# State space layer with tokens in (step, chunk) order, a buffer of its own for u's evictions, and two weight copies behind the first gelu parts

## The chip, the cores and the metric

The kernel runs on one core of a Trainium2 chip. The time is device microseconds of one execution; 1237.46 us is the median of three runs before (1236.57 to 1237.71). The profile is that of one further execution. TensorE is PE in its rows (its weight load PEld), VectorE DVE, ScalarE ACT, GpSimd POOL; SP is the engine that issues most of the DMAs.

## What is computed

The network has two blocks of two layers and one token batch of 256 by 1024 fp32. Only the first layer, a state space mixer, is touched. It projects to u and z, runs a complex diagonal recurrence over the 256 tokens for each of 64 groups, and gates the result:

```python
proj = h @ w_in
u, z = proj[..., :SSM_WIDTH], proj[..., SSM_WIDTH:]
...
y = y.reshape(bsz, seq, SSM_WIDTH) + d_skip.astype(jnp.float32) * uf
y = jax.nn.gelu(y)
y = y * jax.nn.sigmoid(y @ w_glu.astype(jnp.float32) + b_glu.astype(jnp.float32))
y = y.astype(h.dtype) * jax.nn.silu(z)
return y @ w_out
```

The product with `w_glu` is called the unit here.

## The kernel before

The layer is the method `s5`, the first 160 us of the program. All activations are kept transposed, with 128 channels on the partitions and the 256 tokens along the free axis. The 256 tokens are 64 chunks (index j) of 4 steps (index t), and token number 4j + t stands at place 4j + t.

x is transposed and scaled into `hT` (L657 on DVE, L660 on ACT). `gemm_raw` and `block` (L428, L726) form u and z with unsplit fp32 weights. `ev_u` (L695) multiplies each of u's eight blocks by the row factor `rsb`, turns its tokens from (j t) to (t j), and puts it into a `pg` tile; of these the stage has four. Line 696 stores the block to a DRAM buffer `s5ud`, and `load_u` (L735) reads it back as `s5U`, with steps and channels on the partitions: four loads for channels 0 to 511, four for the rest. From `s5U` PE forms the states' inputs (L796), ACT puts them into `s5V` (L799), and DVE runs the recurrence for the first half of the groups and then for the second (L818 to L844), leaving `s5Xc`.

For each half h, PE forms the output (L857, L874), ACT copies it to `s5Y` (L880, the result copy), eight DMAs store it to `s5yd` (L884), and two loads (L893) bring it back with channels on the partitions. The loop over `b` makes of each load a gelu part: gelu on ACT (L896) into `s5gf`, its fp32r high half `s5gh` on ACT (L901), the low half `s5gl` on DVE (L903), both written in the order (j t) from (t j). There are four parts: 1 and 2 from the first half, 3 and 4 from the second.

A weight of the unit comes as eight tiles of 256 by 512. `wtile` makes each ready: a load (L149), the high copy `hi` on ACT (L158), the low copy `lo` on DVE (L160). Tiles 1 and 2 and tiles 3 and 4 are multiplied with parts 1 and 2, tiles 5 and 6 with part 3, tiles 7 and 8 with part 4 (`gemm_t`, L454 to L456). Tiles 1 to 4 are prepared in the branch `if h == 0` that stands ahead of the loop over the parts. The evacuation `ev_glu` (L916 to L921) forms the gated value m, `split` (L193, L194) its halves `s5mh` and `s5ml`, and `out_rows` multiplies by `w_out` (L165 to L167); its weight tiles w1 to w8 pass through `wtile` too.

Each engine and each DMA queue works in the order of issue. `issue_after` sets where in its own engine's order an instruction stands; what it needs from others is waited for by semaphores.

Of the kernel before, what the change touches and what calls it, by code (L numbers as in the profile page):

```python
# [23 lines left out]
C = 512  # L24
KT = 2
# [25 lines left out]
class Net:  # L51
# [570 lines left out]
    def s5(self, x_in):  # L622
        nc, I = self.nc, self.I
        tt = nc.vector.tensor_tensor
        s5p = self.ctx0.enter_context(self.tc.tile_pool(name="s5p", bufs=1))
        dp = self.ctx0.enter_context(self.tc.tile_pool(name="s5d", bufs=1, space=DRAM))
        ud = dp.tile([1024, 256], F32, name="s5ud")
# [44 lines left out]
        zs = [self.xp.tile([128, 4, 256], F32, tag="x", name=self.nm("s5z")) for _ in range(2)]  # L672
# [4 lines left out]
        rsb = self.sp.tile([128, 256], F32, tag="s5rsb", name="s5rsb", bufs=1)  # L677
# [9 lines left out]
        def spread_r():  # L687
            p = self.small()
            with self.tc.issue_after(self.last_raw.ins):
                nc.tensor.matmul(p[:, :256], ones, dg.rearrange("p t n -> p (t n)"), start=True, stop=True)  # L690
            nc.scalar.activation(rsb, p[:, :256], AF.Copy)

        def ev_u(b, p):
            d = self.tmp([128, 4, 64], "s5u")
            self.last_u = tt(d, p.rearrange("p (j t) -> p t j", t=4), rsb.rearrange("p (j t) -> p t j", t=4), op=ALU.mult)  # L695
            nc.sync.dma_start(ud[b * 128:(b + 1) * 128, :], d.rearrange("p t j -> p (t j)"))

        def ev_z(b, p):
            nc.scalar.activation(zs[b // 4][:, b % 4], p, AF.Copy)
# [76 lines left out]

        V = s5p.tile([128, 4096], F32, tag="s5X", name="s5V").rearrange("p (h g q i n) -> p h g q i n", h=2, q=2, i=2, g=4)

        Xc = s5p.tile([128, 2, 2, 2, 8, 65], F32, name="s5Xc")
        nc.gpsimd.memset(Xc[:, :, :, :, :, 0:1].rearrange("p h q c a o -> p (h q c a) o"), 0.0)  # L780
        zg = deque()
        for h in range(2):
# [1 line left out]
        for q in range(2):  # L784
# [84 lines left out]
        for h in range(2):  # L869
# [13 lines left out]
                    r = q * 64 + t * 16  # L883
                    nc.sync.dma_start(yv[q, t][:, 16 * h:16 * h + 16], Y[h][r:r + 16].rearrange("p a g j -> p (a g) j"))  # L884
            if h == 0:
                self.split_after = ly, ls
                order = (0, 4, 2, 6)
                Wg = I["ssm_w_glu"][0]
                for k0, n0 in list(itertools.product(order, (0, C)))[:4]:
                    self.pre.append(self.wtile(Wg[k0 * 128:(k0 + KT) * 128, n0:n0 + C], KT, C, False))  # L890
            for b in (2 * h, 2 * h + 4):
                y = self.tmp([128, 2, 4, 64], "s5y")
                nc.sync.dma_start(y.rearrange("p b t j -> p b (t j)"), yw[:, b:b + 2])  # L893
                i = b % 4
                g = gf[b // 4][:, i:i + 2]
                nc.scalar.activation(g, y, AF.Gelu_apprx_tanh)  # L896
                gh, gl = gT[b // 4]
                if b == 6:
                    lg0, ll0 = lg, ll
                nat = lambda a: a[:, i:i + 2, :].rearrange("p b (j t) -> p b t j", t=4)  # L900
                lg = nc.scalar.activation(nat(gh), g, AF.Copy)  # L901
                with self.tc.issue_after(ls.ins):
                    ll = nc.vector.tensor_tensor(nat(gl), g, nat(gh).bitcast(F32), op=ALU.subtract)  # L903
        self.split_after = lg0, ll0
        for h in range(2):
            with self.tc.issue_after(ll.ins):
# [7 lines left out]
        def ev_glu(b, p):  # L914
            th = self.tmp([128, 256], "s5th")
            nc.scalar.activation(th, p, AF.Tanh, bias=hb[:, b:b + 1], scale=0.5)  # L916
            m = self.tmp([128, 256], "s5mm")
            nc.vector.tensor_tensor(m.rearrange("p (j t) -> p t j", t=4), gf[b // 4][:, b % 4],
                                    zs[b // 4][:, b % 4].rearrange("p (j t) -> p t j", t=4), op=ALU.mult)
            nc.vector.scalar_tensor_tensor(m, zt[b // 4][:, b % 4], 1.0, m, op0=ALU.add, op1=ALU.mult)  # L920
            nc.vector.scalar_tensor_tensor(m, th, 1.0, m, op0=ALU.add, op1=ALU.mult)  # L921
            mh, ml = (a[:, b % 4, :] for a in mT[b // 4])
            self.split(mh, ml, m, 0.25)
        zt = [self.page([128, 4, 256], "s5zt") for _ in range(2)]

        def tanh(h):
# [599 lines left out]
```

## Time and profile before

| | before |
|---|---|
| median of three runs | 1237.46 us |
| the profiled execution, its own time | 1238.92 us |
| its span, first to last instruction | 1237.1 us |
| PE busy | 1205.6 us (97%) |
| DVE busy | 927.1 us (75%) |
| ACT busy | 669.2 us (54%) |
| granted TensorE clock, mean | 0.991 |

The span is the time from the first to the last instruction; the execution's own time has 1.8 us around it. A share of busy time is a mean over stages with different limits, so what the state space layer's 160 us hang on is read from its own stretch of the timelines. A timeline row gives the start in us, the length, engine and line, operation, output and inputs, how many instructions it merges, and in brackets how long the engine stood idle before it and whom it waited for.

### The profile page before, as it was taken

Reading aid. Unit: us, or ns where it says so; the run is one execution under the profiler, and the core shown is the slowest. Engines: PE = TensorE matmul, PEld = TensorE weight load, DVE = VectorE, ACT = ScalarE, POOL = GpSimd, SP = SyncE. Lnnn points to the kernel's source line nnn. Section 1 sums busy time; section 2 is a strip of 40 time slices with the busy share of each in tenths; the row PEclk is TensorE's granted clock in tenths of the full one; section 3 lists DMA queues with packets and bytes.
Section 4 is the critical chain, followed back from the end, with each engine's and each line's share of the span. In section 5 each row is a group of like instructions: output and inputs, shape, how many; then the busy total and the mean of one; then the engine's idle time right before and its main releaser. Section 6 shows DMA issues by size and latency. Waiting matters only on the chain.

```text
span 1237.1 us, 17677 instructions
## 1 busy us (share of the span) xinstructions
PE 1205.6 (97%) x6438; PEld 1000.9 (81%) x6438; DVE 927.1 (75%) x1856; ACT 669.2 (54%) x1137; POOL 8.3 (1%) x29
## 2 busy tenths in 40 slices
PE   7997999999999999999999999999999999999997
PEld 6886887878887888887888887887788887888886
DVE  8895989786899997767654546899998866655544
ACT  5214677765767545446544535668545546544541
POOL 0100000000000000000000000000000000000000
PEclk9898999999999999999999999999999999999999
DMA  8664575443654554663764763744544563765661
GB/s 310 132 95 137 179 225 184 153 141 100 199 167 126 167 170 154 188 204 102 254 188 146 242 204 95 229 136 143 182 146 161 179 210 104 241 192 156 216 201 49
DMA packets 125367, 210.58 MB, mean 170 GB/s; under 512 B 22113, under 2 KB 31329, under 8 KB 125281
## 3 DMA queue, kind: packets, MB, share of 16 engines
q1 hardware_dynamic: 121344, 205.29, 54.0%
q10 hardware_dynamic: 3936, 4.18, 1.1%
q8 instruction: 50, 0.82, 0.3%
q14 instruction: 37, 0.30, 0.1%
HBM read 205.83 MB, written 3.60 MB: 169 GB/s over the span
## 4 chain that ended last, share of the span: by engine, by line
PE 79%; DVE 11%; DMA 4%; ACT 3%; issue 2%; SPq 1%; DVEq 0%; ACTq 0%
PE mm L165 23%; PE mm L167 23%; PE mm L166 23%; DVE lo L160 2%; PE sm L203 2%; ACT hi L158 1%; DVE s5f L818 1%; PE sm L1266 1%; DVE cacc L1018 1%; PE sm L1155 1%; PE sm L1186 1%; DVE s5V L840 1%; PE sm L796 1%; DMA s5bc<-in_c_s 1%; DMA s5ud<-pg 1%
## 5 line engine op out<-in xcount | busy, mean ns | idle before, releaser
L160 DVE TENSOR_TENSOR lo<-raw,hi 128x1024 fp32r<-128x1024 f32 (+2 forms) x372 | 439.9, 1187 | 225.0 <-ACT hi L158 220.6
L158 ACT ACTIVATE hi<-raw 128x1024 fp32r<-128x1024 f32 (+2 forms) x372 | 382.4, 1033 | 358.5 <-PE mm L167 291.0
L165 PE MATMUL mm<-hi,xTh 128*128 128x512 f32 (+2 forms) x1152 | 449.7, 393 | 1.7 <-ACT xTh L193 1.5
L167 PE MATMUL mm<-hi,xTl 128*128 128x512 f32 (+2 forms) x1152 | 442.2, 385 | 0.3 <-DVE t L297 0.2
L166 PE MATMUL mm<-lo,xTh 128*128 128x512 f32 (+2 forms) x1152 | 442.2, 384 | 0.2 <-DVE lo L160 0.2
L165 PEld LDWEIGHTS mm<-hi,xTh 128*128 128x128 f32 x1152 | 216.6, 188 | 49.6 <-ACT xTh L193 7.3
L167 PEld LDWEIGHTS mm<-hi,xTl 128*128 128x128 f32 x1152 | 216.6, 188 | 44.2 <-DVE t L297 1.5
L166 PEld LDWEIGHTS mm<-lo,xTh 128*128 128x128 f32 x1152 | 216.9, 188 | 39.6 <-DVE lo L160 0.5
L1018 DVE SCALAR_TENSOR_TENSOR cacc<-aT,colp,cacc 128x256 f32<-128x256 f32 x240 | 104.7, 478 | 0.0
L165 PE MATMUL mm<-hi,fh 128*128 128x512 f32 x176 | 68.7, 390 | 0.0
L167 PE MATMUL mm<-hi,fl 128*128 128x512 f32 x176 | 68.5, 389 | 0.0
L166 PE MATMUL mm<-lo,fh 128*128 128x512 f32 x176 | 68.5, 389 | 0.0
L167 PEld LDWEIGHTS mm<-hi,fl 128*128 128x128 f32 x176 | 33.0, 188 | 6.9
L166 PEld LDWEIGHTS mm<-lo,fh 128*128 128x128 f32 x176 | 33.1, 188 | 6.8
L165 PEld LDWEIGHTS mm<-hi,fh 128*128 128x128 f32 x176 | 33.1, 188 | 6.7
L194 DVE SCALAR_TENSOR_TENSOR xTl<-sm,colp,xTh 128x128 fp32r<-128x128 f32 x80 | 24.3, 345 | 3.5 <-ACT xTh L193 2.9
L277 DVE SCALAR_TENSOR_TENSOR pg<-mm,post 128x512 f32<-128x512 f32 x16 | 11.0, 690 | 21.1 <-ACT pg L275 21.1
L454 PE MATMUL mm<-s5gh,hi 128*128 128x256 f32 x64 | 19.0, 304 | 7.1 <-ACT s5gh L901 7.1
L956 ACT ACTIVATE pg<-mm,t 128x512 f32<-128x512 f32 x24 | 16.5, 688 | 16.6 <-PE mm L167 16.6
L193 ACT ACTIVATE xTh<-sm,colp 128x128 fp32r<-128x128 f32 x80 | 24.3, 380 | 1.8 <-DVE xTl L194 1.7
L275 ACT ACTIVATE pg<-mm 128x512 f32<-128x512 f32 x16 | 9.5, 596 | 25.5 <-PE mm L167 25.5
L1444 ACT ACTIVATE pg<-mm,t 128x512 f32<-128x512 f32 (+1 forms) x24 | 15.6, 652 | 14.1 <-PE mm L167 14.1
(383 smaller groups left out, 1424.7 us busy)
## 6 DMA issues: line engine op xcount, KB each, us to landing
raw<-in_w_in SPq DMA_DIRECT2D x112, 512.0 KB, 3.5
raw<-in_ffn_w_down SPq DMA_DIRECT2D x44, 512.0 KB, 4.3
raw<-in_ffn_w_gate SPq DMA_DIRECT2D x40, 512.0 KB, 4.5
raw<-in_ffn_w_up SPq DMA_DIRECT2D x40, 512.0 KB, 3.8
raw<-in_attn_w_in SPq DMA_DIRECT2D x32, 512.0 KB, 4.6
raw<-in_ret_w_o SPq DMA_DIRECT2D x16, 512.0 KB, 3.3
raw<-in_w_out SPq DMA_DIRECT2D x16, 512.0 KB, 3.4
raw<-in_ssm_w_glu SPq DMA_DIRECT2D x8, 512.0 KB, 5.6
```

Source lines behind the costliest of these rows:

```text
L158: nc.scalar.activation(h, r, AF.Copy)
L160: self.last_lo = nc.vector.tensor_tensor(l, r, h.bitcast(F32), op=ALU.subtract)
L165: nc.tensor.matmul(out, xh, wh, start=first, stop=False)
L166: nc.tensor.matmul(out, xh, wl, start=False, stop=False)
L167: nc.tensor.matmul(out, xl, wh, start=False, stop=last)
L193: a = nc.scalar.activation(dh, src, AF.Copy if isinstance(scale, float) else AF.Identity, scale=scale)
L194: self.last_split = a, nc.vector.scalar_tensor_tensor(dl, src, scale, dh.bitcast(F32), op0=ALU.mult, op1=ALU.subtract)
L203: nc.tensor.transpose(pt[:, b * 128:(b + 1) * 128], row[:, (b0 + b) * 128:(b0 + b + 1) * 128], self.ident)
L454: nc.tensor.matmul(o, wh, xh, start=first and b % 2 == 0, stop=False, skip_group_check=True)
L956: nc.scalar.activation(gate[t, n], p, AF.Tanh, scale=hf(t))
L1018: nc.vector.scalar_tensor_tensor(cacc[:, b, :], src, sc, cacc[:, b, :], op0=ALU.mult, op1=ALU.add)
L1444: nc.scalar.activation(sg[t][:, :nn], p, AF.Silu, scale=rstd[:, t:t + 1])
```

## The change

Tokens stand in (t j) order from `hT` to m: the evictions of `hT` read PSUM in steps of four, `rsb` is turned once, `ev_u` and the gelu halves and the first product of m are dense, and only m's halves are written back to the order (j t). `ev_u` writes into eight places of a buffer `ue`, which lies in the room that `Xc` uses later, and the stores of blocks 4 to 7 are issued behind the first four `load_u`. The loads of tiles 3 and 4 go behind the two loads of parts 1 and 2; their copies go behind these parts, the last high copy behind the second half's result copy.

```diff
-                o, pi, g = hT[b // 4][:, b % 4 + i], pt[:, i * 256:i * 256 + 256], g0[:, b + i:b + i + 1]
+                o, pi, g = hT[b // 4][:, b % 4 + i].rearrange("p (t j) -> p t j", t=4), pt[:, i * 256:i * 256 + 256].rearrange("p (j t) -> p t j", t=4), g0[:, b + i:b + i + 1]
...
-            nc.scalar.activation(rsb, p[:, :256], AF.Copy)
+            nc.scalar.activation(rsb.rearrange("p (t j) -> p t j", t=4), p[:, :256].rearrange("p (j t) -> p t j", t=4), AF.Copy)
...
-            d = self.tmp([128, 4, 64], "s5u")
-            self.last_u = tt(d, p.rearrange("p (j t) -> p t j", t=4), rsb.rearrange("p (j t) -> p t j", t=4), op=ALU.mult)
-            nc.sync.dma_start(ud[b * 128:(b + 1) * 128, :], d.rearrange("p t j -> p (t j)"))
+            d = ue[:, b]
+            self.last_u = tt(d, p, rsb, op=ALU.mult)
+            with self.tc.issue_after(self.load_after.ins) if b > 3 else ExitStack():
+                nc.sync.dma_start(ud[b * 128:(b + 1) * 128, :], d)
...
-                for k0, n0 in list(itertools.product(order, (0, C)))[:4]:
-                    self.pre.append(self.wtile(Wg[k0 * 128:(k0 + KT) * 128, n0:n0 + C], KT, C, False))
...
+                for j in range(2):
+                    load(j, self.load_after)
+                    high(j, ly)
+                low(0, ls)
+            else:
+                high(3, ly)
+                low(3, ls)
...
-                nat = lambda a: a[:, i:i + 2, :].rearrange("p b (j t) -> p b t j", t=4)
+                nat = lambda a: a[:, i:i + 2, :].rearrange("p b (t j) -> p b t j", t=4)
...
+            if h == 0:
+                for j in (2, 3):
+                    load(j, ld)
+                high(2, lg)
+                low(1, ll)
+                low(2, ll)
...
-            nc.vector.tensor_tensor(m.rearrange("p (j t) -> p t j", t=4), gf[b // 4][:, b % 4],
-                                    zs[b // 4][:, b % 4].rearrange("p (j t) -> p t j", t=4), op=ALU.mult)
+            nc.vector.tensor_tensor(m, gf[b // 4][:, b % 4].rearrange("p t j -> p (t j)"), zs[b // 4][:, b % 4], op=ALU.mult)
...
-            mh, ml = (a[:, b % 4, :] for a in mT[b // 4])
-            self.split(mh, ml, m, 0.25)
+            mh, ml = (a[:, b % 4, :].rearrange("p (j t) -> p t j", t=4) for a in mT[b // 4])
+            self.split(mh, ml, m.rearrange("p (t j) -> p t j", t=4), 0.25)
```

On ACT, where the first half's gelu parts meet the weight copies (`s5gf` a gelu, `s5gh` its high half, `hi` a weight's high copy, `s5Y` the second half's result copy), the order before is:

```order
L861 ACTIVATE t_155_1006<-sm_971 128x8
L158 ACTIVATE hi_1129<-raw_1128 128x1024
L158 ACTIVATE hi_1135<-raw_1134 128x1024
L896 ACT_TABLE_LOAD
L896 ACTIVATE s5gf_1012<-pg_1140 128x512
L901 ACTIVATE s5gh_1008<-s5gf_1012 128x2x4x64
L896 ACTIVATE s5gf_1013<-pg_1145 128x512
L901 ACTIVATE s5gh_1010<-s5gf_1013 128x2x4x64
L880 ACTIVATE s5Y_895<-sm_970 128x8x64
L880 ACTIVATE s5Y_895<-sm_971 128x8x64
```

and after:

```order
L864 ACTIVATE t_147_999<-sm_964 128x8
L920 ACT_TABLE_LOAD
L920 ACTIVATE s5gf_1005<-pg_1120 128x512
L925 ACTIVATE s5gh_1001<-s5gf_1005 128x512
L920 ACTIVATE s5gf_1006<-pg_1125 128x512
L925 ACTIVATE s5gh_1003<-s5gf_1006 128x512
L902 ACTIVATE hi_1131<-raw_1130 128x1024
L883 ACTIVATE s5Y_888<-sm_963 128x8x64
L883 ACTIVATE s5Y_888<-sm_964 128x8x64
L902 ACTIVATE hi_1135<-raw_1134 128x1024
```

The high copies of tiles 3 and 4 stood ahead of both parts; now tile 3's stands behind them, and tile 4's behind the result copy.

On SP, from the stores of the first half's output (`s5yd`) to those of the second, with the loads of the parts (`pg`) and of weight tiles 3, 4, 5, ... (`raw`), the order before is:

```order
L884 DMA s5yd<-s5Y_894 16x16x64 x8
L149 DMA raw_1128<-in_ssm_w_glu 128x2x512
L149 DMA raw_1134<-in_ssm_w_glu 128x2x512
L893 DMA pg_1140<-s5yd 128x2x256
L893 DMA pg_1145<-s5yd 128x2x256
L149 DMA raw_1346<-in_ssm_w_glu 128x2x512
L149 DMA raw_1376<-in_ssm_w_glu 128x2x512
L149 DMA raw_1406<-in_ssm_w_glu 128x2x512
L149 DMA raw_1436<-in_ssm_w_glu 128x2x512
L884 DMA s5yd<-s5Y_895 16x16x64 x8
L893 DMA pg_1224<-s5yd 128x2x256
```

and after:

```order
L887 DMA s5yd<-s5Y_887 16x16x64 x8
L917 DMA pg_1120<-s5yd 128x2x256
L917 DMA pg_1125<-s5yd 128x2x256
L897 DMA raw_1130<-in_ssm_w_glu 128x2x512
L897 DMA raw_1134<-in_ssm_w_glu 128x2x512
L149 DMA raw_1339<-in_ssm_w_glu 128x2x512
L149 DMA raw_1369<-in_ssm_w_glu 128x2x512
L887 DMA s5yd<-s5Y_888 16x16x64 x8
L917 DMA pg_1217<-s5yd 128x2x256
```

The loads of parts 1 and 2 moved ahead of weight loads 3 and 4, and of the weight loads ahead of the second half's stores four are left (tiles 3 to 6) where there were six.

On SP in the first part, with u's stores (`s5ud`), the last weight load of z and the loads of `s5U`, the order before is:

```order
L696 DMA s5ud<-pg_343 128x256
L412 DMA raw_341<-in_ssm_w_in 128x2x512
L696 DMA s5ud<-pg_346 128x256
L696 DMA s5ud<-pg_349 128x256
L696 DMA s5ud<-pg_352 128x256
L696 DMA s5ud<-pg_405 128x256
L696 DMA s5ud<-pg_417 128x256
L735 DMA s5U<-s5ud 16x32x64 x4
```

and after:

```order
L698 DMA s5ud<-s5ue 128x256
L412 DMA raw_342<-in_ssm_w_in 128x2x512
L698 DMA s5ud<-s5ue 128x256 x3
L738 DMA s5U<-s5ud 16x32x64 x4
L698 DMA s5ud<-s5ue 128x256 x4
```

Two of u's stores no longer stand ahead of the first loads of `s5U`.

## Rows read from the trace of the kernel before

**Rows 1.** PE's timeline, around the unit and in the first part.

```profile
100.38 2.08 PE L874 MATMUL sm<-s5Xc,s5cab 64*64 64x64 f32 x64 [1.12 <-DVE s5Xc L844]
109.57 1.01 PE L454 MATMUL mm<-s5gh,hi 128*128 128x256 f32 x3 [7.11 <-ACT s5gh L901]
...
135.52 0.28 PE L456 MATMUL mm<-s5gh,lo 128*128 128x256 f32 x1
...
142.03 0.50 PE L167 MATMUL mm<-hi,s5ml 128*128 128x512 f32 x1 [0.17 <-DVE s5ml L194]
...
45.55 5.64 PE L796 MATMUL sm<-s5U,s5W 64*64 64x64 f32 x128 [1.92 <-DMA s5U<-s5ud]
...
56.26 3.95 PE L796 MATMUL sm<-s5U,s5W 64*64 64x64 f32 x128
```

**Rows 2.** Stretches: busy us of PE, PEld, DVE, ACT, POOL; granted clock; DMA share, GB/s.

```profile
48.00:50.00 2.00, 2.00 (x43) 2.00 (x42) 1.86 (x10) 0.89 (x2) 0.00 (x0) 0.50 1.20 107
...
100.00:102.00 2.00, 1.62 (x54) 1.62 (x56) 2.00 (x3) 0.00 (x0) 0.00 (x0) 1.00 0.00 0
...
112.00:114.00 2.00, 2.00 (x11) 2.00 (x11) 0.27 (x1) 0.01 (x1) 0.00 (x0) 0.50 0.47 90
...
116.00:118.00 2.00, 2.00 (x20) 2.00 (x18) 0.00 (x0) 0.00 (x0) 0.00 (x0) 1.00 0.81 129
```

**Rows 3.** ACT's timeline from the end of the recurrence to part 3.

```profile
97.01 1.06 ACT L158 ACTIVATE hi<-raw 128x1024 fp32r<-128x1024 f32 x1
105.39 1.06 ACT L158 ACTIVATE hi<-raw 128x1024 fp32r<-128x1024 f32 x1 [7.32 <-DMA raw<-in_ssm_w_glu]
106.46 1.28 ACT L896 ACT_TABLE_LOAD   x1
...
108.42 1.10 ACT L901 ACTIVATE s5gh<-s5gf 128x512 fp32r<-128x512 f32 x1
...
110.91 1.10 ACT L880 ACTIVATE s5Y<-sm 128x512 f32<-128x512 f32 x2
120.12 0.63 ACT L896 ACTIVATE s5gf<-pg 128x512 f32<-128x512 f32 x1 [8.11 <-DMA pg<-s5yd]
```

**Rows 4.** SP's timeline: DMA issues, the length being the time of issue.

```profile
89.17 12.70 SPq L149 DMA_DIRECT2D raw<-in_ssm_w_glu  x2
...
112.03 5.05 SPq L884 DMA_DIRECT2D s5yd<-s5Y  x8
117.25 1.99 SPq L893 DMA_DIRECT2D pg<-s5yd  x2
...
32.45 0.37 SPq L696 DMA_DIRECT2D s5ud<-pg  x1
...
38.89 1.96 SPq L735 DMA_DIRECT2D s5U<-s5ud  x4
```

**Rows 5.** Issue to landing (last, us): issued at 101.48, 113.45, 117.25, 32.45.

```profile
raw<-in_ssm_w_glu SPq DMA_DIRECT2D x1, 512.0 KB, 3.9
...
s5yd<-s5Y SPq DMA_DIRECT2D x1, 64.0 KB, 3.5
...
pg<-s5yd SPq DMA_DIRECT2D x1, 256.0 KB, 2.9
...
s5ud<-pg SPq DMA_DIRECT2D x1, 128.0 KB, 5.9
```

**Rows 6.** DVE's timeline: the recurrence's start and end, and the unit.

```profile
62.83 0.29 DVE L827 TENSOR_TENSOR pg<-pg,s5dk 128x128 f32<-128x128 f32 x1 [1.12 <-ACT pg L774]
...
100.24 3.49 DVE L160 TENSOR_TENSOR lo<-raw,hi 128x1024 fp32r<-128x1024 f32 x3
...
121.97 1.15 DVE L903 TENSOR_TENSOR s5gl<-s5gf,s5gh 128x512 fp32r<-128x512 f32 x1 [9.70 <-ACT s5gh L901]
...
133.28 1.15 DVE L918 TENSOR_TENSOR pg<-s5gf,s5z 128x256 f32<-128x256 f32 x2
134.35 0.75 DVE L920 SCALAR_TENSOR_TENSOR pg<-s5zt,pg 128x256 f32<-128x256 f32 x2
...
137.32 0.75 DVE L194 SCALAR_TENSOR_TENSOR s5ml<-pg,s5mh 128x256 fp32r<-128x256 f32 x2
```

More of the change, by code (lines that the diff above doesn't have):

```diff
@@ L690, in spread_r @@
                 nc.tensor.matmul(p[:, :256], ones, dg.rearrange("p t n -> p (t n)"), start=True, stop=True)
-            nc.scalar.activation(rsb, p[:, :256], AF.Copy)
+            nc.scalar.activation(rsb.rearrange("p (t j) -> p t j", t=4), p[:, :256].rearrange("p (j t) -> p t j", t=4), AF.Copy)
         def ev_u(b, p):
-            d = self.tmp([128, 4, 64], "s5u")
-            self.last_u = tt(d, p.rearrange("p (j t) -> p t j", t=4), rsb.rearrange("p (j t) -> p t j", t=4), op=ALU.mult)
-            nc.sync.dma_start(ud[b * 128:(b + 1) * 128, :], d.rearrange("p t j -> p (t j)"))
+            d = ue[:, b]
+            self.last_u = tt(d, p, rsb, op=ALU.mult)
+            with self.tc.issue_after(self.load_after.ins) if b > 3 else ExitStack():
+                nc.sync.dma_start(ud[b * 128:(b + 1) * 128, :], d)
+        ue = s5p.tile([128, 4160], F32, tag="s5Xc", name="s5ue")[:, :2048].rearrange("p (b n) -> p b n", b=8)
         def ev_z(b, p):
@@ L777, in s5 @@
         V = s5p.tile([128, 4096], F32, tag="s5X", name="s5V").rearrange("p (h g q i n) -> p h g q i n", h=2, q=2, i=2, g=4)
-        Xc = s5p.tile([128, 2, 2, 2, 8, 65], F32, name="s5Xc")
+        Xc = s5p.tile([128, 4160], F32, tag="s5Xc", name="s5Xc").rearrange("p (h q c a k) -> p h q c a k", h=2, q=2, c=2, a=8)
         nc.gpsimd.memset(Xc[:, :, :, :, :, 0:1].rearrange("p h q c a o -> p (h q c a) o"), 0.0)
@@ L885, in s5, with load, high, low @@
             if h == 0:
-                self.split_after = ly, ls
                 order = (0, 4, 2, 6)
                 Wg = I["ssm_w_glu"][0]
-                for k0, n0 in list(itertools.product(order, (0, C)))[:4]:
-                    self.pre.append(self.wtile(Wg[k0 * 128:(k0 + KT) * 128, n0:n0 + C], KT, C, False))
+                early = []
+                def load(j, after):
+                    k0, n0 = order[j // 2], j % 2 * C
+                    early.append([self.wbuf(t) for t in ("raw", "hi", "lo")])
+                    with self.tc.issue_after(after.ins):
+                        nc.sync.dma_start(early[j][0], Wg[k0 * 128:(k0 + KT) * 128, n0:n0 + C].rearrange("(k p) n -> p k n", p=128))
+                    self.pre.append(early[j][1:])
+                def high(j, after):
+                    with self.tc.issue_after(after.ins):
+                        nc.scalar.activation(early[j][1], early[j][0], AF.Copy)
+                def low(j, after):
+                    raw, hi, lo = early[j]
+                    with self.tc.issue_after(after.ins):
+                        self.last_lo = nc.vector.tensor_tensor(lo, raw, hi.bitcast(F32), op=ALU.subtract)
+                for j in range(2):
[5 more added lines that the diff above has]
+                low(3, ls)
             for b in (2 * h, 2 * h + 4):
                 y = self.tmp([128, 2, 4, 64], "s5y")
-                nc.sync.dma_start(y.rearrange("p b t j -> p b (t j)"), yw[:, b:b + 2])
+                ld = nc.sync.dma_start(y.rearrange("p b t j -> p b (t j)"), yw[:, b:b + 2])
                 i = b % 4
```

## The prediction

> **What bounds the kernel now.** Only the state space layer changes, so I read its timelines, PE's first. Its recurrence ends with the matmuls of the second half's output, which start at 100.38 and last 2.08 us, to 102.46. Then PE stands still for 7.11 us and starts the unit's 192 matmuls at 109.57; the last begins at 135.52 [rows 1]. The clock makes the idle time dearer: at 112 to 114 us the granted clock is 0.50 (1.2 GHz of 2.4), and only at 116 to 118 it is 1.00 again [rows 2].
>
> Next, what PE waited for: the high half of part 1 on ACT. ACT reaches the copies at 97.01, when tile 3's high copy runs, and then waits 7.32 us for the load of tile 4; only behind that copy (105.39) come the table load and parts 1 and 2. The second half's result copy, whose matmuls ended at 102.46, stands behind them all and begins at 110.91, 8.45 us late [rows 3].
>
> Why is load 4 late? SP's row of the two weight loads is 12.70 us long, from 89.17 to 101.87 [rows 4]: by the built program's waits load 4 needs a buffer that tile 1's low copy frees, and DVE gets to that copy at 100.24, when the recurrence is over [rows 6]. All that time the loads of parts 1 and 2 stand behind it on SP.
>
> The late result copy sets the rest. Its stores are issued from 112.03, part 3's load at 117.25 [rows 4]; ACT waits 8.11 us for it and starts the gelu at 120.12 [rows 3]. DVE waits 9.70 us for the part's high half, works from 121.97 almost without pause, and reaches the first low halves of m at 137.32 [rows 6]. PE's last wait for those is at 142.03 [rows 1]; behind it the product with w_out fills PE. So the way from 102 to 142 us is bound by what stands in front on ACT and SP, not by work.
>
> **The second half of the layer, step by step.** Times are those of the trace before; a shift of the first part comes off afterwards.
>
> 1. SP is free for the parts' loads at 89.17 instead of 101.97. They need the first half's stores landed; with 2.9 us of their own [rows 5] they are there by some 95 us, before ACT can use them. Load 3 lands about 4 us behind them (3.9 us, [rows 5]), load 4 as before behind tile 1's low copy.
> 2. ACT is free at 97.01. Table load 1.28, two gelus of 0.63 [rows 3], two high halves. Those were 1.10 with a strided output [rows 3]; dense I take 0.6, the gelu's own price at the same size. With tile 3's copy at 1.06 the sum is 97.0 + 1.3 + 2.5 + 1.1 = 101.9, before the matmuls end. The result copy runs from 102.5 to 103.6 instead of 110.91 to 112.0: 8.4 us earlier.
> 3. The new place has its own wait. On SP four weight loads stand ahead of the second half's stores, and by the program's waits the last, load 6, needs tile 2's low copy, which now stands on DVE behind the low halves of parts 1 and 2. DVE: low copy 1 from 100.24, 1.16 (3.49 / 3 [rows 6]); two low halves, 1.15 strided before [rows 6], dense some 0.7 (two instructions of half the size take 0.75 [rows 6]); low copy 2: 100.24 + 1.16 + 1.4 + 1.16 = 104.0. Queued behind it are the eight stores, hence part 3: they start at 104.4, not at the result copy's 103.6, at a cost of 0.8 us.
> 4. The eight stores take 5.05 us of issue [rows 4], and also wait for landings: the sixth, seventh and eighth for loads 4, 5 and 6 (they reuse their semaphores). Load 4 issued at 101.5 lands at 105.4, load 6 at 104.0 some 3.9 us later, at 107.9, about when the eighth store's turn comes. So issue ends at 109.4, and part 3's load goes out there instead of at 117.25: 7.8 us earlier. It lands 2.9 us on, at 112.3. Bounds: 108.4 if the row's one long store does not recur, and 112 if each store lands as slowly as u's store did under weight loads (5.9 against 3.5 us [rows 5]).
> 5. From gelu 3 to m's low halves it took 120.12 to 137.32, 17.2 us, and DVE filled 15.35 of it. Dense halves take 0.6 off the wait ahead of DVE (its high half 1.10 to 0.6 and small change) and 0.45 off each of two low halves; the first product of m, twice 256 elements strided, falls from 1.15 to 0.75 [rows 6]. That is 1.9, and a wait of about 0.1 less for w_out's third tile, whose load follows earlier copies: 15.2 us. So 112.3 + 15.2 = 127.5 instead of 137.32: **9.8 us earlier**.
> 6. Does PE keep up? It can start at 102.5, behind its own matmuls: part 1 and tile 1 are ready at 102.1. Before it needed 26.1 us (109.57 to 135.6), of which at most half of the 6 us at the lower level is lost, so 23 to 26. Tile 5's low copy comes about 1.4 us after tile 4's products are done. End 126.9 to 128.6, before the product with w_out gets its low halves and the three matmuls ahead of them. PE is no new bound.
> 7. The halves of m become strided, eight blocks in four rounds. The low halves' nearest row is the old first product of m, which has the same strides: +0.40 a pair, and that product gives 0.40 back. The bounds are 0 and +0.40 a round, 0 to 1.6 in all; I take 0. The high halves grow by some 0.24 each (half of 1.10 less 0.63), on an ACT that waits for DVE there: nothing, and some 0.2 a round if that cover is gone.
>
> A page of the Trainium skill speaks against step 7: "Vector Engine (DVE) Microarchitecture Reference", section 5.2, "Measured stream behaviour on trn2 (trn3 not measured)", gives about 2.5 ns an element for small steps that touch no neighbour, where dense streams need 1.05. By that, if the product gave back only its row's 0.40, four rounds would lose an estimated 1.4 us and the time would be 1228.6. The strided low half, 512 elements in 1.15 us [rows 6], does not bear out so high a price.
>
> **The first part.** The fourth of u's stores, issued at 32.45, landed 5.9 us later at 38.35 [rows 4, 5]; the first four `s5U` loads need only stores 1 to 4 but went out at 38.89, behind stores 5 and 6. They can go 0.4 us earlier, and PE's L796, which waited 1.92 us for them at 45.55, with them. DVE no longer waits for `pg` tiles and its evictions become dense, some 3 us, but it meets the next wait anyway: at 62.83 it stands idle 1.12 us for the taps that PE and ACT deliver [rows 6], and they follow L796 in PE's order. What is late next is thus PE, and the part gives **0.4 us**; bounds 0 (the loads land together with the weight loads around them) and 2 (below). u's last four stores move behind the `s5U` loads; their own loads feed the second L796 at 56.26, behind other matmuls, so 1 to 2 us later costs nothing. The strided PSUM reads of `hT` and `rsb` have no row on ACT. If each of the seven costs 0.24 more (strided against dense above) it is 1.7 us, and below nothing there is no gain, since nothing in them is removed. I take 0: DVE's 3 us cover them, uncovered they would cost at most 1.7.
>
> Sum: 9.8 + 0.4 = 10.2 us. Against the profiled execution: span 1237.1 - 10.2 = 1226.9, own time 1238.92 - 10.2 = 1228.7. The median of the runs lies 1.46 below that execution's own time, so the forecast is 1237.46 - 10.2 = **1227.3 us**. Behind the layer nothing has a fixed place in time, so the gain should last to the end.
>
> **Rivals.** *The stores land late* (step 4's upper bound, 112 instead of 109.4, or one more wait of that size): part 3 comes 3 us later and DVE's chain with it. For it: loads 4, 5 and 6 and the stores share one queue within 4 us; against: before, four loads stood there. Time 1230.3.
>
> *TensorE's level in the first part.* After 1.92 us of idling L796 ran at 0.50 (48 to 50 us) and took 5.64 us, its twin at full level 3.95 [rows 1, 2]. If L796 keeps the upper level behind a gap that is 0.4 us shorter, 1.7 us come back there, and some of the product behind it: 2 us, since u's second loads arrive only shortly before. Time 1225.3. The Trainium skill says in "TensorE: Matmul & The Clock Gate", "What's actually happening", that recent idleness puts the array on the lower level and lasting work lifts it. The trace agrees with both levels, and shows that idle time does not always cost one: L874 waited 1.12 us and ran at 1.00 behind it (100 to 102 us, [rows 1, 2]). The same could hit the unit's start, which moves to matmuls with gaps among them; step 6 shows up to 2.6 us absorbed.
>
> *Slower: load 6 holds the stores.* They stand behind a load that hangs on parts 1 and 2, and these on the first half's loads. Every microsecond that tile 2's low copy comes after 104.0 is passed on whole. From 10 us late the change loses: the loads of parts 1 and 2 would have to land after 107 instead of 95. Then 1241 or more. Against it: ACT only waited for a weight load there, and SP is free from 89.17.
>
> *The change leaves the order as it was*: the built program shows otherwise. What is left is that several of these waits add up to the whole gain.
>
> **How the numbers follow.** Forecast 0.76, with its own range of 1225.0 to 1229.6 (bounds of steps 4 and 7 and of the first part); late stores 0.12; clock kept 0.07; slower 0.03; no difference 0.02. A range of 1224.6 to 1230.6 takes in the first three. What a measurement can tell is about 0.2%, 2.5 us: faster 0.95, within it 0.02, slower 0.03.
>
> **What would show it.** Right, if the unit's first matmul follows the last L877 without a gap and at a clock of 1.00, the result copy starts near 102, the second half's stores near 104, gelu 3 near 112 and m's low halves near 127 (all less 0.4). Wrong in step 3 or 4, if SP's eight stores begin after 105 or take over 6 us; wrong in step 7, if a pair of low halves exceeds 1.2 us and PE waits for them in every round; wrong in the first part, if L799 starts later than 45.6.

## The result, and the profile after

| | before | after |
|---|---|---|
| first measurement, median (lowest to highest) | 1237.59 us (1236.57 to 1239.53, 4 runs) | 1227.50 us (1225.69 to 1230.13, 4 runs) |
| ratio, 95% interval | | 0.9914 (0.9895 to 0.9932) |
| all measurements, median (lowest to highest) | 1237.76 us (1234.96 to 1241.50, 54 runs) | 1228.90 us (1225.69 to 1230.84, 9 runs) |
| profiled execution: own time, span | 1238.92, 1237.1 us | 1230.13, 1228.3 us |

Forecast were 1227.3 us, a gain of 10.2. The first measurement says 10.1. The two profiled executions differ by 8.8, the medians of all runs by 8.9. So the sign, the place and the range were right; the layer's second half, as the traces below show, gave 8.2 and 8.75 us where 9.8 were forecast.

In the changed kernel L799 is the old L796, L877 the old L874, L883 the result copy, L887 its stores, L897, L902 and L907 load, high copy and low copy of tiles 1 to 4, L917 the loads of the parts, L920, L925 and L927 gelu, high half and low half, L948 to L950 the products of m.

PE's timeline after (start, length, operation, idle time before it and whom it waited for), answering [rows 1]:

```profile
45.04 5.74 PE L799 MATMUL sm<-s5U,s5W 64*64 64x64 f32 x128 [1.44 <-DMA s5U<-s5ud]
...
99.84 2.08 PE L877 MATMUL sm<-s5Xc,s5cab 64*64 64x64 f32 x64 [1.11 <-DVE s5Xc L847]
101.86 0.63 PE L454 MATMUL mm<-s5gh,hi 128*128 128x256 f32 x3
...
127.73 0.50 PE L165 MATMUL mm<-hi,s5mh 128*128 128x512 f32 x1 [0.70 <-ACT s5mh L193]
...
129.04 0.50 PE L167 MATMUL mm<-hi,s5ml 128*128 128x512 f32 x1 [0.58 <-DVE s5ml L194]
...
131.96 0.50 PE L165 MATMUL mm<-hi,s5mh 128*128 128x512 f32 x1 [0.35 <-ACT s5mh L193]
```

The 7.11 us of idle time ahead of the unit are gone: its first matmul follows L877 directly. Stretches after, as in [rows 2] (the third number from the right is the granted clock):

```profile
46.00:48.00 2.00, 2.00 (x56) 2.00 (x53) 1.90 (x8) 1.19 (x2) 0.00 (x0) 0.68 0.32 72
48.00:50.00 2.00, 2.00 (x44) 2.00 (x42) 1.90 (x7) 0.60 (x2) 0.00 (x0) 0.50 0.82 131
...
102.00:104.00 2.00, 2.00 (x18) 2.00 (x19) 2.00 (x3) 1.04 (x2) 0.00 (x0) 1.00 0.87 268
112.00:114.00 2.00, 1.63 (x14) 1.43 (x12) 0.37 (x1) 1.67 (x3) 0.00 (x0) 1.00 1.01 281
```

At 112 to 114 us TensorE now runs at its upper level, where it stood at 0.50; at 48 to 50 it is at 0.50 as before. ACT's and SP's timelines after, answering [rows 3] and [rows 4]:

```profile
96.62 1.28 ACT L920 ACT_TABLE_LOAD   x1
97.91 0.63 ACT L920 ACTIVATE s5gf<-pg 128x512 f32<-128x512 f32 x1
98.58 0.63 ACT L925 ACTIVATE s5gh<-s5gf 128x512 fp32r<-128x512 f32 x1
...
101.96 1.09 ACT L883 ACTIVATE s5Y<-sm 128x512 f32<-128x512 f32 x2 [0.62 <-PE sm L877]
...
112.30 0.63 ACT L920 ACTIVATE s5gf<-pg 128x512 f32<-128x512 f32 x1 [6.70 <-DMA pg<-s5yd]
...
116.18 0.63 ACT L920 ACTIVATE s5gf<-pg 128x512 f32<-128x512 f32 x1 [0.68 <-DMA pg<-s5yd]
```

```profile
88.30 2.08 SPq L917 DMA_DIRECT2D pg<-s5yd  x2
90.42 10.90 SPq L897 DMA_DIRECT2D raw<-in_ssm_w_glu  x2
101.37 2.34 SPq L149 DMA_DIRECT2D raw<-in_ssm_w_glu  x2
103.75 5.37 SPq L887 DMA_DIRECT2D s5yd<-s5Y  x8
109.68 0.38 SPq L917 DMA_DIRECT2D pg<-s5yd  x1
110.10 0.48 SPq L149 DMA_DIRECT2D raw<-in_ssm_w_glu  x1
111.08 0.36 SPq L917 DMA_DIRECT2D pg<-s5yd  x1
```

The parts' loads go out at 88.30, ACT comes to the gelu without a wait, the result copy starts when its matmuls end, and the stores 1.8 us later. Part 3's gelu starts 7.8 us earlier than before, m's low halves (the fourth row below) 9.0 us. DVE's timeline after, answering [rows 6], and ahead of it the time from issue to landing (last number) of the loads issued at 109.68 and 111.08:

```profile
pg<-s5yd SPq DMA_DIRECT2D x1, 256.0 KB, 2.6
...
pg<-s5yd SPq DMA_DIRECT2D x1, 256.0 KB, 5.1
```

```profile
113.63 0.69 DVE L927 TENSOR_TENSOR s5gl<-s5gf,s5gh 128x512 fp32r<-128x512 f32 x1 [6.77 <-ACT s5gh L925]
...
117.79 1.23 DVE L160 TENSOR_TENSOR lo<-raw,hi 128x1024 fp32r<-128x1024 f32 x1 [0.85 <-ACT hi L158]
...
125.21 0.76 DVE L948 TENSOR_TENSOR pg<-s5gf,s5z 128x256 f32<-128x256 f32 x2
...
128.36 1.17 DVE L194 SCALAR_TENSOR_TENSOR s5ml<-pg,s5mh 128x256 fp32r<-128x256 f32 x2
...
132.59 1.17 DVE L194 SCALAR_TENSOR_TENSOR s5ml<-pg,s5mh 128x256 fp32r<-128x256 f32 x2
```

The layer's end in the trace is the residual sum behind the product with `w_out`; its last pair on DVE before and after:

```profile
160.24 1.28 DVE L285 TENSOR_TENSOR x<-mm,x 128x512 f32<-128x512 f32 x2
```

```profile
151.48 1.28 DVE L285 TENSOR_TENSOR x<-mm,x 128x512 f32<-128x512 f32 x2
```

That is 8.76 us, the whole difference of the spans: nothing was given back behind the layer.

**A measure for the runs below.** Runs of one kernel spread over 5 us, so most edits are read from their traces, in four terms: *start*, when the second half's output matmuls (L877) begin; from there to *gelu 3*; from gelu 3 to *m's low halves*; from there to the *sum* at the layer's end. All in us, each from the four rows named; "level" says whether TensorE fell to 0.50 in the first part of that execution.

| kernel | start | to gelu 3 | to m's low halves | to the sum | start to sum | level |
|---|---|---|---|---|---|---|
| before | 100.38 | 19.74 | 17.20 | 22.92 | 59.86 | fell |
| after | 99.84 | 12.46 | 16.06 | 23.12 | 51.64 | fell |
| e1_both | 97.00 | 12.67 | 15.33 | 23.11 | 51.11 | stayed |
| e2_tokens | 97.84 | 18.92 | 16.04 | 23.15 | 58.11 | stayed |
| e3_copies | 98.11 | 12.71 | 16.48 | 22.95 | 52.14 | stayed |
| e4_ue | 99.51 | 20.01 | 17.20 | 22.94 | 60.15 | fell |
| e5_late_low | 97.22 | 13.13 | 15.28 | 23.13 | 51.54 | stayed |
| e6_loads_only | 96.83 | 18.14 | 16.02 | 23.12 | 57.28 | stayed |
| e7_part4_first | 96.94 | 12.06 | 15.94 | 23.13 | 51.13 | stayed |
| e8_gap | 96.76 | 12.60 | 13.75 | 23.35 | 49.70 | stayed |
| e9_dose | 99.71 | 14.74 | 15.33 | 23.13 | 53.20 | fell |
| e10_fill | 97.76 | 12.30 | 15.38 | 23.14 | 50.82 | stayed |
| e11_gap_fill | 97.60 | 12.83 | 14.67 | 23.34 | 50.84 | stayed |
| e12_before_fill | 98.00 | 19.21 | 16.71 | 22.92 | 58.84 | stayed |

### The profile page after: what moved, and what is told of

The parts are those of the page before. It is cut to its first block, busy times and chain, and to the rows that moved or that the text cites. A ratio compares the mean times of both kernels' runs of the same rounds, so it can differ in the third digit from the quotient of the medians.

```text
span 1228.3 us, 17673 instructions
## 1 busy us (share of the span) xinstructions
PE 1203.4 (98%) x6438; PEld 998.7 (81%) x6438; DVE 923.4 (75%) x1856; ACT 669.2 (54%) x1137; POOL 8.3 (1%) x29
## 4 chain that ended last, share of the span: by engine, by line
PE 83%; DVE 9%; DMA 3%; ACT 2%; issue 2%; SPq 0%; DVEq 0%; ACTq 0%
PE mm L165 25%; PE mm L167 24%; PE mm L166 24%; PE sm L203 2%; DVE lo L160 1%; PE sm L1184 1%; PE sm L1295 1%; DVE s5f L821 1%; ACT hi L158 1%; PE sm L1215 1%; DVE s5V L843 1%; PE sm L799 1%; PE sm L1203 1%; PE sm L1177 1%; PE sm L1283 1%
## 5 line engine op out<-in xcount | busy, mean ns | idle before, releaser
L160 DVE TENSOR_TENSOR lo<-raw,hi 128x1024 fp32r<-128x1024 f32 (+2 forms) x368 | 435.0, 1186 | 223.0 <-ACT hi L158 221.6
L158 ACT ACTIVATE hi<-raw 128x1024 fp32r<-128x1024 f32 (+2 forms) x368 | 378.4, 1033 | 347.6 <-PE mm L167 288.0
L821 DVE TENSOR_TENSOR s5f<-s5V,s5E 128x1024 f32<-128x1024 f32 x16 | 18.9, 1225 | 2.0 <-ACT s5V L802 1.8
```

The source lines that it names most:

```text
L158: nc.scalar.activation(h, r, AF.Copy)
L160: self.last_lo = nc.vector.tensor_tensor(l, r, h.bitcast(F32), op=ALU.subtract)
L821: tt(p[o], V[:, h, None, :, q, o].to_broadcast(sh), self.E[:, e:e + 2, q, 8 * h:8 * h + 8].rearrange("p c a k -> p c (a k)")[:, :, None, : ...
```

## The experiments

**The change once more, e1_both**, the changed kernel as it is.

> The changed kernel once more, beside before in the same rounds. The theory of the prediction (9.8 us in the second half of the layer, 0.4 in the first part) expects a ratio of 0.9918 with bounds 0.990 and 0.994. The trace of the first profiled execution shows a span shorter by 8.8 us only, so the rival is that about 8.5 us is the true gain: ratio 0.9931.

Measured: 1229.49 us (1226.72 to 1230.84), ratio 0.9937 (0.9922 to 0.9952). The rival's 8.5 us are what this measurement gives; its profiled execution, at 1226.72, is 3.4 us shorter than the first profiled one of the same program. Of these 3.4 us 2.84 lie in the first part. PE's timeline of e1, then its stretch from 46 to 48 us:

```profile
44.57 3.95 PE L799 MATMUL sm<-s5U,s5W 64*64 64x64 f32 x128 [0.98 <-DMA s5U<-s5ud]
```

```profile
46.00:48.00 2.00, 2.00 (x76) 2.00 (x73) 1.90 (x8) 1.39 (x3) 0.00 (x0) 1.00 0.30 66
```

Here TensorE stays at the upper level, L799 takes 3.95 us instead of 5.74, and L877 starts 2.84 us earlier. So the spread of one kernel's runs is in good part a matter of this level, and e10 to e12 test it.

The mean granted clock, which is on record for most timed runs, sorts them in the same way. Of the kernel before, 25 runs stand at 0.992 or less (median 1239.34 us) and 25 at 0.994 or more (1236.82). Of the changed kernel, five stand at 0.996 or less (1230.13) and four at 0.998 or more (1226.59). The traced executions fit: with the fall 0.991 before and 0.996 after, without it 0.999 in e1. At like level the gain is thus 9.2 or 10.2 us. Three of the first measurement's four runs of the changed kernel stand in its upper group and one of e1's five, while the runs of before beside e1 are split 11 to 12. So the 10.1 us of the one and the 8.5 of the other differ in part by the level that their runs happened to have.

**One part alone: e2_tokens.** Only the token order; copies, loads and u's buffer as before.

```diff
-                o, pi, g = hT[b // 4][:, b % 4 + i], pt[:, i * 256:i * 256 + 256], g0[:, b + i:b + i + 1]
+                o, pi, g = hT[b // 4][:, b % 4 + i].rearrange("p (t j) -> p t j", t=4), pt[:, i * 256:i * 256 + 256].rearrange("p (j t) -> p t j", t=4), g0[:, b + i:b + i + 1]
...
-            d = self.tmp([128, 4, 64], "s5u")
...
+            d = self.tmp([128, 256], "s5u")
+            self.last_u = tt(d, p, rsb, op=ALU.mult)
```

> Token order alone; weight copies, loads and u's buffer as before. Theory: the late result copy stays where it was, behind the high copy of tile 4; it comes 1.0 us earlier since the two dense high halves ahead of it are 0.5 shorter each, and the dense work between gelu 3 and m's low halves gives 1.9: 2.9 us, 1234.6 us (ratio 0.9977, bounds 0.996 and 1.000). Rival, that strided writes of m's halves cost more than the first product gives back (four rounds, 1.4 us): 1236.0. Rival, that the token order carries the main part of the gain: under 1232.

Measured: 1235.53 us, ratio 0.9980 (0.9969 to 0.9992); start to sum 1.75 us shorter. Gelu 3 comes 0.82 earlier (1.0 expected), but the way from there to m's low halves shrinks by 1.16 only where 1.9 were expected. DVE shows why:

```profile
119.03 1.23 DVE L160 TENSOR_TENSOR lo<-raw,hi 128x1024 fp32r<-128x1024 f32 x1 [0.26 <-ACT hi L158]
120.50 1.23 DVE L160 TENSOR_TENSOR lo<-raw,hi 128x1024 fp32r<-128x1024 f32 x1 [0.24 <-ACT hi L158]
...
131.66 1.23 DVE L160 TENSOR_TENSOR lo<-raw,hi 128x1024 fp32r<-128x1024 f32 x1 [0.51 <-ACT hi L158]
```

The dense halves make DVE faster than ACT, and DVE waits 1.0 us in three places for ACT's high copies, where before it waited 0.41 us in one. The token order does not carry the main part, and the writes of m's halves cost no 1.4 us.

**e3_copies.** Only the moved loads and copies (the block `if h == 0` with `load`, `high` and `low`, as in the change).

> The moved loads and copies alone; tokens and u's buffer as before. Theory: the strided halves stay, so the result copy ends about 1.0 us later than in the changed kernel and tile 2's low copy, which lets load 6 and with it the stores go, 0.9 us later; part 3 comes 7.0 us earlier than before instead of 7.8, and nothing is gained from there to m's low halves; the load of part 4, which stands behind weight load 7, costs up to 0.9. So 6 to 7 us, 1230.5 to 1231.5 (ratio 0.9943 to 0.9952). Rival, that the copies alone carry all: 1227.7.

Measured: 1229.74 us (1227.73 to 1231.30), ratio 0.9933 (0.9918 to 0.9948). By totals it cannot be told from the whole change; by the trace it gives 7.72 of 8.22 to 8.75 us. ACT:

```profile
100.22 1.09 ACT L880 ACTIVATE s5Y<-sm 128x512 f32<-128x512 f32 x2 [0.33 <-PE sm L874]
...
110.82 0.63 ACT L917 ACTIVATE s5gf<-pg 128x512 f32<-128x512 f32 x1 [7.07 <-DMA pg<-s5yd]
```

The result copy starts 2.11 us behind L874 (10.53 before), and gelu 3 comes 7.03 us earlier, as expected. The 0.9 us for the late load of part 4 were not lost here: DVE, with its strided halves, has no wait between the low halves of parts 3 and 4. From gelu 3 to m's low halves, where nothing was expected, 0.72 us are gained, mainly since DVE's wait of 0.41 us for w_out's third tile is gone.

**e4_ue.** Only u's own buffer and the later stores.

```diff
-            d = self.tmp([128, 4, 64], "s5u")
...
+            d = ue[:, b]
...
+            with self.tc.issue_after(self.load_after.ins) if b > 3 else ExitStack():
+                nc.sync.dma_start(ud[b * 128:(b + 1) * 128, :], d)
```

> Only the buffer of its own for u's evictions, with the later stores of blocks 4 to 7. Theory: the first loads of s5U go out 0.4 us earlier and the states' inputs start 0.4 us earlier on PE: 1237.1, ratio 0.9997 (bounds 0.998 and 1.000). The wait of DVE for a free buffer is gone, and DVE then waits longer at the taps. Rival, that PE keeps its upper clock level there: 1235.5.

Measured: 1236.51 us, ratio 0.9994 (0.9983 to 1.0005): inconclusive by totals; at like level the medians are 0.9 and 1.3 us under those of before. The second half's output matmuls start 0.87 us earlier than before, in two executions in which the level fell; in the five kernels with this buffer whose level stayed and that have no fill (e1, e5 to e8) they start at 96.76 to 97.22, in the two without it (e2, e3) at 97.84 and 98.11.

**What held the result copy: e6_loads_only.** The changed kernel, with the parts' loads ahead of weight loads 3 and 4, but the copies ahead of the parts as before.

```diff
+                for j in (2, 3):
+                    load(j, ld)
+                    high(j, ly)
+                for j in (1, 2, 3):
+                    low(j, ls)
...
+                with self.tc.issue_after(self.last_hi.ins):
+                    nc.scalar.activation(g, y, AF.Gelu_apprx_tanh)
```

> The changed kernel with the loads of weight tiles 3 and 4 behind the parts' loads on SP, as changed, but all four high copies ahead of parts 1 and 2 on ACT and the four low copies ahead of their low halves on DVE, as before. Theory (what held the result copy was ACT's order): ACT waits for load 4 again, until about 105; table load, two gelus and two dense high halves follow, and the result copy starts near 109.5 instead of 101.96. The gain is what token order and u's buffer give, some 2.5 to 3.3 us: ratio 0.9975. Rival (the parts' loads behind weight load 4 on SP were the cause): result copy before 104, ratio 0.993.

Measured: 1232.97 us, ratio 0.9956 (0.9941 to 0.9972). ACT's timeline:

```profile
101.36 1.06 ACT L902 ACTIVATE hi<-raw 128x1024 fp32r<-128x1024 f32 x1 [6.80 <-DMA raw<-in_ssm_w_glu]
...
106.10 1.06 ACT L883 ACTIVATE s5Y<-sm 128x512 f32<-128x512 f32 x2
```

With L877 at 96.83, the result copy starts 9.27 us behind it, against 2.12 in the changed kernel and 10.53 before. Start to sum is 57.28, a gain of 2.58 as the theory said. The total gains more, 5.6 us by the medians: all five runs, at 0.995 and 0.996, are on the upper level in the first part, as the trace is, and eight of the twelve runs of before beside them are not. Against the upper group of before (1236.82) it is 3.9 us. SP's order without ACT's gives little, 0.83 us from start to sum against e2; ACT's order, the high copy that waits for load 4, was the cause. ACT's order without SP's was not run: with the parts' loads issued at 101.97, as before, ACT could not have had part 1 ahead of that.

**Does load 6 hold the stores? e5_late_low and e9_dose.** Both put low copies later on DVE with SP's order held. In e5 it was tile 2's.

```diff
                 low(3, ls)
+                low(1, ls)
...
-                low(1, ll)
```

> The changed kernel with tile 2's low copy put on DVE behind those of tiles 3 and 4, and SP's order held as in the changed kernel, load 6 ahead of the second half's stores. Theory of step 3 (load 6 waits for that copy and holds the stores): low copy 2 ends near 108 instead of 103.2, SP's eight stores begin near 108.4 instead of 103.75, part 3's gelu starts 4.6 us later than in the changed kernel, m's low halves too, and the time is 4 to 5 us over the changed kernel's: ratio to before about 0.997. Rival (the stores hang on the result copy and the queue): the stores begin near 104 as before this edit and only PE loses, waiting 3 us for tile 2's low copy: at most 2 us over the changed kernel.

Measured: 1229.88 us, ratio 0.9937 (0.9916 to 0.9958); the stores begin 3.85 us behind L877, as in the changed kernel (3.91). DVE's low copy of tile 3, then SP:

```profile
99.42 1.22 DVE L908 TENSOR_TENSOR lo<-raw,hi 128x1024 fp32r<-128x1024 f32 x1
```

```profile
88.22 12.81 SPq L898 DMA_DIRECT2D raw<-in_ssm_w_glu  x4
101.07 5.93 SPq L888 DMA_DIRECT2D s5yd<-s5Y  x8
```

The edit did not set the dose: by the waits of this built program load 6 took the buffer of tile 3, whose low copy had moved forward, and went out at 100.66, right behind that copy's end at 100.64. So it tells nothing about the wait. e9 puts both behind tile 4's.

```diff
-                low(3, ls)
+                for j in (3, 1, 2):
+                    low(j, ls)
```

> The changed kernel with the low copies of tiles 2 and 3 behind that of tile 4 on DVE, load 6 held ahead of the second half's stores. Load 6 then needs the buffer that tile 4's low copy frees. Theory of step 3: that copy ends about 6.8 us after the start of the second half's output matmuls (L877), so the eight stores begin 7.2 us after that start instead of 3.9, part 3's gelu some 15.8 us after it instead of 12.5 to 12.7, and the table load of the next layer's norm 70.5 to 71 us after it instead of 67.1 to 67.8. Rival (the stores hang on the result copy, which ends 3.2 us after that start): they begin at 3.5 to 4 us, and only PE's waits for the late low copies show.

Measured: 1229.67 us, ratio 0.9945 (0.9925 to 0.9965). SP and ACT:

```profile
90.28 16.90 SPq L898 DMA_DIRECT2D raw<-in_ssm_w_glu  x4
107.22 4.25 SPq L888 DMA_DIRECT2D s5yd<-s5Y  x8
```

```profile
101.82 1.09 ACT L883 ACTIVATE s5Y<-sm 128x512 f32<-128x512 f32 x2 [0.62 <-PE sm L877]
...
114.45 0.63 ACT L922 ACTIVATE s5gf<-pg 128x512 f32<-128x512 f32 x1 [8.93 <-DMA pg<-s5yd]
```

The stores begin 7.51 us behind L877 (99.71) though the result copy was done 3.2 behind it: load 6 holds them, and the rival falls. But gelu 3 comes only 2.28 us later, not 3.3: the eight stores then take 4.25 us to issue instead of 5.37, probably since most of the loads whose semaphores they reuse have landed by then. The wait is passed on, though not whole; start to sum is 53.20, 1.6 to 2.1 us over the changed kernel's.

**e7_part4_first.** Weight load 7 behind part 4's load.

```diff
-                for j in (2, 3):
+                for j in range(2, 6):
...
+        self.load_after = ld
```

> The changed kernel with part 4's load put ahead of weight load 7 on SP. Theory (step 5 lost 0.9 us because part 4 comes 3.9 us behind part 3, not 2.6 as before): gelu 4 starts about 1.5 us behind gelu 3, DVE's pauses of 0.25 and 0.85 us between the low halves of parts 3 and 4 go, m's low halves come 15.2 us behind gelu 3 instead of 16.06, and the time falls by 0.9. Rival (DVE waits for weight load 7 or 8 in their place): no change.

Measured: 1231.09 us (1227.53 to 1232.87), ratio 0.9937 (0.9920 to 0.9955); gelu 4 comes 2.15 us behind gelu 3, yet m's low halves come 15.94 behind it. DVE's pauses are now 0.25, 0.25 and 0.39 us, the last one for the high copy of w_out's third tile. So the rival's "no change" holds, though DVE waits for another tile than the rival had named. DVE's row:

```profile
123.79 1.22 DVE L160 TENSOR_TENSOR lo<-raw,hi 128x1024 fp32r<-128x1024 f32 x1 [0.39 <-ACT hi L158]
```

**Using the pause: e8_gap.** e7 with both copies of tiles 5 and 6 and the scaling of z in the time in which ACT and DVE wait for part 3.

```diff
-                high(3, ly)
-                low(3, ls)
+                for j in range(3, 6):
+                    high(j, ly)
+                    low(j, ls)
+                self.z_after = self.last_lo
...
-            with self.tc.issue_after(ll.ins):
+            with self.tc.issue_after(self.z_after.ins):
```

> The changed kernel with part 4's load ahead of weight load 7, and with both copies of tiles 5 and 6 and the scaling of z put into the time in which ACT and DVE wait for part 3 (6.7 us each). Theory: DVE has 4.7 us less to do between gelu 3 and m's low halves; PE becomes the bound there and runs the unit's 192 matmuls without a pause, 23.0 us from 101.9, to 124.9 instead of 127.0, and the 2 us of waits in the first rounds of the product with w_out go too: 3.5 us under the changed kernel (bounds 2 and 4.5), ratio to before 0.990. Rival (the copies wait for load 6 so long that they delay gelu 3 or its low half): gain under 1 us or a loss.

Measured: 1226.64 us (1225.49 to 1231.00), ratio 0.9914 (0.9895 to 0.9934). Start to sum is 49.70, 1.4 to 1.9 us under the changed kernel, half of what was expected. By totals the intervals of the two overlap, and at like level its medians (1225.87 and 1229.86) are 0.7 and 0.3 us under the changed kernel's, so it is better by its trace alone. DVE, then PE:

```profile
107.92 2.35 DVE L940 TENSOR_TENSOR s5z<-s5z,s5rsb 128x1024 f32<-128x1024 f32 x2
...
114.85 2.36 DVE L160 TENSOR_TENSOR lo<-raw,hi 128x1024 fp32r<-128x1024 f32 x2 [2.15 <-ACT hi L158]
...
123.11 1.17 DVE L194 SCALAR_TENSOR_TENSOR s5ml<-pg,s5mh 128x256 fp32r<-128x256 f32 x2
```

```profile
122.69 0.40 PE L165 MATMUL mm<-hi,s5mh 128*128 128x512 f32 x1
```

Of the 4.7 us taken off DVE, 2.15 came back as a wait for tile 7's high copy. PE begins the product with w_out 25.9 us behind L877's start instead of 27.4 (e1) to 27.9: in this trace a gain of the unit is there. e11 below does not repeat it.

**The level: e10_fill, e11_gap_fill, e12_before_fill.** Six matmuls whose result nobody reads, ahead of L799, in the changed kernel, in e8's and in the kernel before.

```diff
+        idle = self.small()
+        for k in range(6):
+            lf = nc.tensor.matmul(idle[:, :256], ones, xs[0], start=True, stop=True)
```

> The changed kernel with six matmuls of 128x256, whose result is not used, between PE's L610 and the states' inputs L799: they fill 1.3 us of the 1.0 to 1.7 us in which PE waits for s5U. Theory (PE's level falls at L799 in some executions because PE stood idle ahead of it): L799 takes 3.95 us in every execution, all runs lie near the lower end of the changed kernel's spread, 1226 to 1227.5, and the spread of 5 us shrinks under 2. Rival (the small 64x64 matmuls themselves bring the fall, or it has another cause): the runs spread from 1226 to 1231 as before.

> The kernel of e8_gap with the same six matmuls ahead of L799. Theory: near 1225 in all executions, ratio to before 0.989; under the rival of e10_fill as e8_gap, median 1226.6 with a spread of 5 us.

> The kernel before with the same six matmuls ahead of its L796. Theory: if the two levels account for the spread of the kernel before too, its runs gather near the lower end, 1235 to 1236.5, ratio 0.998. Rival: no change, 1235 to 1241, median 1238.

Measured: e10 1228.04 us (1226.65 to 1229.08), ratio 0.9922 (0.9910 to 0.9935); e11 1227.38 (1226.76 to 1228.38), 0.9919 (0.9905 to 0.9932); e12 1235.31 (1234.59 to 1237.30, 11 runs), 0.9982 (0.9973 to 0.9991). The kernel before spread from 1235.87 to 1240.69 beside them. PE in e10, then in e12:

```profile
43.44 2.76 PE L768 MATMUL sm<-s5x,s5one 128*128 128x256 f32 x12
46.12 3.95 PE L802 MATMUL sm<-s5U,s5W 64*64 64x64 f32 x128
```

```profile
43.13 2.75 PE L765 MATMUL sm<-s5x,s5one 128*128 128x256 f32 x12
45.82 3.95 PE L799 MATMUL sm<-s5U,s5W 64*64 64x64 f32 x128
```

The fill takes 2.76 us, twice what was planned, so L799 starts 1.1 us later than in the first trace after. Still the level stays in all three traces, and the granted clock of all 20 runs is that of the upper groups (0.997 or more in e10 and e11, 0.994 or more in e12). The runs of each kernel spread over 1.6 to 2.7 us, and the old kernel gains 2.2 us by its medians in that measurement. The fill has effects of its own: against the upper group of its own kernel e10 is 1.4 us longer and e12 1.5 us shorter. Why they differ is not shown.

e11 shows no gain over e8's median, and from start to sum none over e10 (50.84 against 50.82). Beside fill, e8's edit gives nothing: DVE waits twice for high copies there.

```profile
116.04 1.23 DVE L160 TENSOR_TENSOR lo<-raw,hi 128x1024 fp32r<-128x1024 f32 x1 [2.15 <-ACT hi L158]
...
118.26 3.78 DVE L160 TENSOR_TENSOR lo<-raw,hi 128x1024 fp32r<-128x1024 f32 x3 [0.99 <-ACT hi L158]
```

So the gain of e8 stands on one trace. With the level held in both, e10 and e12 differ by 7.3 us; of that start to sum gives 8.0 and the start 0.24, and about 1 us comes back behind the layer in these two traces, where 1076.7 to 1077.9 us from the sum to the span's end were seen in all traces but e9's, in which the level fell once more at 182 to 188 us.

## Why the prediction was right, and where it was not

- **What bounds** was read rightly. e6 shows that ACT's order held the result copy, as [rows 3] told, and that SP's move by itself gives little (0.83 us).
- **Steps 1 and 2** hold to 0.5 us: the parts' loads at 88.30 (89.17 less the shift of 0.4 forecast), result copy at 101.96 (102.5 less 0.4), dense high halves 0.63.
- **Step 3** holds: stores at 103.75 (104.4 less 0.4 forecast). Load 6 went out at 103.34, right behind tile 2's low copy. e9 shows the wait for load 6 itself; that it is passed on whole, as the slower rival had it, is not so (2.28 of 3.60 us). That rival's load of parts 1 and 2 went out at 88.30; nothing of it happened.
- **Step 4** was sized short in both traces of the changed kernel, by 0.5 us in the first and 0.75 in e1. The stores took 5.37 us to issue (5.05 of [rows 4] taken), and part 3's load then waited 0.56 more for them to land, which the step had left out; the load itself was 0.3 shorter. From L877 to gelu 3 it is 12.46 us, forecast was 11.92; in e1 it is 12.67, with 5.47 us of issue and 0.53 of waiting.
- **Step 5** was short by 0.86 us in the first trace after (16.06, forecast 15.2) and by 0.13 in e1 (15.33). In the first, part 4's load, behind weight load 7 on SP, takes 5.1 us where part 3's takes 2.6, and DVE waits 0.25 and 0.85 us for high copies; in e1 part 4's load takes 4.4, and DVE waits 0.26. The shares of the step were wrong in both. It put 1.9 us down to DVE's shorter instructions and 0.1 to a shorter wait for w_out's third tile, and left ACT's and SP's shares as they were. By e2 the shorter instructions alone give 1.16, since DVE then waits 1.0 us for high copies, 0.6 more than before; by e3 the moved copies alone give 0.72. That the two together make e1's 1.87, close to the 2.0 forecast, is luck. e7 brings part 4 earlier and gains nothing: the waits for high copies stay.
- **Step 6** holds: the unit starts without a gap at 1.00, and its last matmul ends at 127.0, forecast were 126.9 to 128.6 (0.4 less with the shift).
- **Step 7** holds: a pair of low halves went from 0.75 to 1.17, the product from 1.15 to 0.76, and a round lasts 4.23 us instead of 4.21. Behind them 0.2 to 0.4 us are lost in every kernel with the token order (23.11 to 23.35 against 22.92 to 22.95): PE waits 0.35 us for the second round's strided high half, the cover that the step had named. The estimate of 1.4 us that the prediction worked out from the Trainium skill ("Vector Engine (DVE) Microarchitecture Reference", section 5.2) is not borne out.
- **The first part** gave 0.54 us, forecast was 0.4; where the level stayed, e1 starts 0.84 and 1.11 us ahead of e2 and e3, which lack u's buffer.

Sum of the first trace after: 7.28 + 1.14 - 0.20 + 0.54 = 8.76, where 7.8 + 2.0 + 0 + 0.4 = 10.2 were forecast. In e1 the second half gives 7.07 + 1.87 - 0.19 = 8.75. That the first four runs gave 10.1 all the same was in part luck: by the granted clock three of them were on the upper level, where half of the runs of before are on the lower. At like level the change gave 9.2 or 10.2 us.

The rival on TensorE's level was put wrongly, as a result of the change. It is a property of the execution: the level fell in the first traces of before and after, in e4 and e9, and stayed in e1 to e3 and e5 to e8, with the change's buffer and without it, behind waits of PE of 1.15 to 1.92 us in the one group and 0.83 to 1.68 in the other. The Trainium skill says in "TensorE: Matmul & The Clock Gate", "What's actually happening", that recent idleness brings the lower level; that three filled kernels kept it agrees. The length of the wait alone does not sort the traces here.

Open: why the level falls in one execution and not in the next, the 1 us behind the layer between e10 and e12, and whether e8's edit gains anything beyond its one trace.

## What to carry to other kernels

Look in an in-order engine's queue for an instruction that waits for data ahead of one whose data are ready; moving it behind, with the loads that go with it, was worth 7 to 8 us here, and the move of the loads on SP alone under 1. When instructions on one engine are made shorter, price who feeds it first: in e2 0.7 of the 1.9 us expected from the shorter instructions came back, mostly as waits for ACT. Where runs of one kernel spread by more than the edit is worth, compare stretches of the traces between two events, sort the runs by their granted clock, or hold the cause of the spread still in both kernels; and see whether a gain of one trace comes again in a second.

## What was not expected of the hardware

- TensorE's level in the first part differed between executions of one program; the same 128 matmuls took 3.95 us or 5.04 to 5.74, and the second half's output matmuls began 2.84 us apart (after and e1).
- A matmul of 128x256 in fp32 from unsplit operands appears as two in the trace: six took 2.76 us.
- A queue's stores went out faster after a longer wait (4.25 against 5.37 us for eight), probably as the transfers whose semaphores they reuse had landed.
